# Low parts of the weights made by accumulating transfers, and an S5 step with one scan whose state ScalarE copies

## Chip, core and metric

One NeuronCore of a Trainium2 chip runs the whole program. The metric is the device time in microseconds (us) of one execution. The engines are named as the profile names them: PE (TensorE), DVE (VectorE), ACT (ScalarE), POOL (GpSimd), and SP, which here only issues DMA transfers.

## The reference

A hybrid block of two layers works on 512 latent tokens and 256 context tokens of width 1024, in float32. Each layer does an adaptive RMS norm, one wide input projection (`h @ w_in`, 6656 columns), three token mixers of width 512 whose columns come from that projection, a gated merge, an output projection and a residual add:

```python
q, k, v, za, xr, zr, us, zs, gl = split(h @ w_in)
ya = diff_attention(q, k, v)              # 4 heads, differential softmax
yr = rglru(depthwise_conv(xr))            # h[t] = a[t] h[t-1] + b[t], both directions
ys = s5(us)                               # complex diagonal state space, both directions, GLU
y  = [ya * silu(za), yr * silu(zr), ys * silu(zs)]
x  = x + gate * (sum(sigmoid(g) * (y_n @ w_branch_n)) @ w_out)
```

The S5 branch has 32 groups of 16 channels with 64 complex states each. Each state obeys h[t] = a h[t-1] + B u[t] with a constant complex a, once forwards and once backwards over the tokens; latent tokens start from the last state of the context.

## The kernel before

**Products in three parts.** Every weight product runs on PE in a rounded 32-bit format, and each operand is split into a high part and a low part so that the result is float32-like. For activations this gives hH and hL. For weights the helper `wsplit` (line 152) loads a block of 128x512 into `raw`, ACT writes the high part (`wh`, line 160) and DVE subtracts to get the low part:

```python
S.activation(wh, raw, AF.Copy)
V.tensor_sub(wl, raw, f32(wh))
```

`product` (line 164) then runs, for each of four k tiles of a block, the passes wh x hH, wh x hL and wl x hH, each over 512 latent and 256 context tokens: 24 matmuls a block, of which the fifth is the first that reads wl. The tiles wr, wh and wl have three buffers each (the four blocks of the LRU have one).

**The S5 stage.** In each layer the LRU branch (`lru(i)`, four of them), gate projections, `merge_y`, the first branch projection and the 16 steps of S5 are interleaved as the table PLAN says. In the first layer this stage follows the projection of the S5 input, at about 85 us, and ends at about 390 us; in the second it lies about 1030 to 1240 us. In the first layer the S5 tables and weights are made within the stage, on DVE (lines 442 to 515); in the second they are loaded.

**One S5 step.** The sequence is cut into 96 chunks of 8 tokens, so a scan runs over 96 elements. `s5_scan(pa)` (line 592) handles two groups in both directions. 16 matmuls on PE write the chunk inputs px (line 601), 128 partitions (two groups of 64 states) by 2 x 2 x 96 (real and imaginary, two directions). On DVE: the inputs are turned by the angle table into xx (lines 611 to 614), four real scans with the constant decay rho run in place, one for each direction and part (line 618), and the result is turned back: U2 and W2 (lines 623 and 624), then four half-height operations write the state tile st, which has real parts in partitions 0 to 63 and imaginary ones in 64 to 127 for one group each:

```python
V.tensor_sub(st[0:64, g, ...], U2[ps, 0, ...], W2[ps, 1, ...])      # line 628, g = 0, 1
V.tensor_add(st[64:128, g, ...], U2[ps, 1, ...], W2[ps, 0, ...])    # line 629
```

In the first layer one more copy (line 631) repeats 32 columns of st. `s5_out(pa)` (line 633) multiplies st and the inputs on PE into ps_y; ACT copies that to yo (line 647) and SP stores it. `step(pa)` issues the scan of pa + 1 ahead of the output of pa; there are two st tiles, one xx.

**Order.** Each engine runs its own list of instructions in order. The lists are laid down when the program is built, by the framework's planner, which may put independent instructions of one engine in another order than the program text has: in the trace parts of an S5 step stand between parts of an LRU. Transfers are issued by SP, which is also an in-order list, or by POOL. In the first layer's S5 stage POOL issues nothing; it issues transfers later, when the second layer's S5 tables are stored (lines 452 to 527).

Of the kernel before, what the change touches and what calls it, by code (L numbers as in the profile page):

```python
# [11 lines left out]
F32 = mybir.dt.float32  # L12
F32R = mybir.dt.float32r
AF = mybir.ActivationFunctionType
OP = mybir.AluOpType
# [14 lines left out]
NCH = 96  # L30
NCC = 32
# [20 lines left out]
def hybrid_kernel(ctx, tc, xT, cc, wmod, win, winv, wbr, wout, wglu, wlru, par, lqk, s5a, s5b, s5B, s5C, dsk, rope, outT):  # L52
    nc = tc.nc
    V, S, G, PE, SP = nc.vector, nc.scalar, nc.gpsimd, nc.tensor, nc.sync
# [30 lines left out]
    def f32(ap):  # L85
        return ap.bitcast(F32)
# [20 lines left out]
    ones = pC.tile([128, 32], F32, name="ones")  # L107
# [41 lines left out]
        return mods[:, l, 4 + k // 4, k % 4, c:c + 1]  # L149


    def wsplit(src, n, p=None, bufs=3, keep=None):
        p = p or pW
        raw = p.tile([128, 512], F32, name="wr", tag="wr", bufs=bufs)
        if keep:
            p, bufs = keep, None
        wh = p.tile([128, 512], F32R, name="wh", tag="wh", bufs=bufs)
        wl = p.tile([128, 512], F32R, name="wl", tag="wl", bufs=bufs)
        SP.dma_start(raw, src)
        S.activation(wh, raw, AF.Copy)  # L160
        V.tensor_sub(wl, raw, f32(wh))  # L161
        return wh.rearrange("p (k n) -> p k n", n=n), wl.rearrange("p (k n) -> p k n", n=n)

    def product(blocks, rhs, segs, out, first=True, last=True):
# [72 lines left out]
    rho = pC.tile([128, L * 32], F32, name="rho")  # L237
# [310 lines left out]
    def s5_make(l):  # L548
        need = l < L - 1
        s5st, p5 = pool(f"s5{l}", 1, side="right")  # L550
        usd = pD.tile([512, 8, NCE], F32, name=f"usd{l}")
        yd = pD.tile([512, 8, NCH], F32, name=f"yd{l}")
        NCL = NCH if need else NCH - NCC
        sts = [p5.tile([128, 2, 2, NCE], F32, name=f"st{i}", tag=f"st{i}") for i in range(2)]
        vts, sps, tps = {}, {}, {}
        if l == 0:
            pr_ = s5_params(l, p5, S5_BUFS, V)
# [34 lines left out]
        def s5_scan(pa):  # L592
            pr = pa % 4
            vt, (tb, ws) = vts[pa // 4], turn(pa)

            px = mis("ps_x")
            for d in range(2):
                for c in range(2):
                    for g in range(2):
                        v = vt[:, 2 * pr + g, :NCH] if d == 0 else vt[:, 2 * pr + g, NCE - 1:NCE - 1 - NCH:-1]  # L600
                        PE.matmul(px[64 * g:64 * g + 64, (c * 2 + d) * NCH:(c * 2 + d + 1) * NCH],  # L601
                                  lhsT=ws[:, 2 * d + g, 64 * c:64 * c + 64], rhs=v, start=True, stop=True)
            pxv = px[:, :4 * NCH].rearrange("p (c d j) -> p c d j", c=2, d=2)

            sh = [128, 2, 2, NCH]
            Cb = tb[:, 0].unsqueeze(1).to_broadcast(sh)
            Sb = tb[:, 1].unsqueeze(1).to_broadcast(sh)
            U = p5.tile([128, 2, 2, NCH], F32, name="U", tag="U")
            Wt = p5.tile([128, 2, 2, NCH], F32, name="W", tag="W")
            xx = p5.tile([128, 2, 2, NCH], F32, name="xx", tag="xx")  # L610
            V.tensor_mul(U, pxv, Cb)
            V.tensor_mul(Wt, pxv, Sb)
            V.tensor_add(xx[:, 0], U[:, 0], Wt[:, 1])
            V.tensor_sub(xx[:, 1], U[:, 1], Wt[:, 0])
            for d in range(2):
                b = l * 32 + 2 * pa + d
                for c in range(2):
                    V.tensor_tensor_scan(xx[:, c, d], rho[:, b:b + 1].to_broadcast([128, NCH]), xx[:, c, d], 0.0,
                                         op0=OP.mult, op1=OP.add)
            U2 = p5.tile([128, 2, 2, NCH], F32, name="U2", tag="U")  # L620
            W2 = p5.tile([128, 2, 2, NCH], F32, name="W2", tag="W")
            js = slice(0 if need else NCC - 1, NCH - 1)
            V.tensor_mul(U2[..., js], xx[..., js], Cb[..., js])
            V.tensor_mul(W2[..., js], xx[..., js], Sb[..., js])
            st = sts[pa % 2]
            for g in range(2):
                ps = slice(64 * g, 64 * g + 64)
                V.tensor_sub(st[0:64, g, :, js.start + 1:NCH], U2[ps, 0, :, js], W2[ps, 1, :, js])
                V.tensor_add(st[64:128, g, :, js.start + 1:NCH], U2[ps, 1, :, js], W2[ps, 0, :, js])
            if need:  # L630
                V.tensor_copy(st[:, :, 0, NCH:], st[:, :, 0, :NCC])

        def s5_out(pa):

# [25 lines left out]
        def ahead():  # L660
            for st in sts:
                V.memset(st[:, :, :, 0:1], 0.0)
            if l > 0:
                for p in range(3):
                    fetch(p)
                return
            whole(pr_.powers())
            s5_inner(0)
            done[0] = 1
            whole(pr_.tables(0))  # L670
# [22 lines left out]
    for l in range(L):  # L693
# [23 lines left out]
        for k in range(KT):  # L717
# [7 lines left out]
            b = pH.tile([128, TT], F32R, name="hL", tag="hL")  # L725
# [52 lines left out]

        if l == 0:
            s5.ahead()  # L780


        def lru(i):
# [131 lines left out]
        for dt in range(KT):  # L915
# [2 lines left out]
            V.scalar_tensor_tensor(m_t[dt][:, :W], m_t[dt][:, :W], 1.0, pb[:, :W], op0=OP.add, op1=OP.mult)  # L918
            gate_early(2, dt)
        s5.close()  # L920


        s5t, p6 = pool(f"s5t{l}", 4, side="right")
# [2 lines left out]
        for i in range(4):  # L926
            a = p6.tile([128, 8, NCL], F32, name="gt", tag="gt")
            SP.dma_start(a, s5.yd[i * 128:(i + 1) * 128, :, :NCL])
            b = p6.tile([128, 8 * NCL], F32R, name="gtH", tag="gtH")
            c = p6.tile([128, 8 * NCL], F32R, name="gtL", tag="gtL")  # L930
# [9 lines left out]
        for n in range(4):  # L940
            wh, wl = wsplit(wglu[l, n].rearrange("p k n -> p (k n)"), 128)
# [80 lines left out]
        for h in range(4):  # L1022
# [5 lines left out]
            for q0 in ([0, 2, 4] if need else [0, 2]):  # L1028
# [5 lines left out]
                for qi in range(2):  # L1034
# [3 lines left out]
                    for c in range(2):  # L1038
# [4 lines left out]
                        for t0, w, c0 in ks:  # L1043
# [12 lines left out]
                                           op1=OP.add)  # L1056
# [246 lines left out]
```

## Time and profile before

| what | value |
|---|---|
| median of 3 runs | 1617.53 us (1614.93 to 1617.88) |
| profiled execution, its own time | 1609.46 us |
| its span, first to last instruction | 1607.6 us |
| busy over the span: PE, DVE, ACT, POOL | 93%, 73%, 47%, 8% |
| mean granted clock of PE | 0.973 of full speed |

A busy share is an average over stages, so it says little about any one of them; the views by stage further down do. "Idle before, releaser" in a row is the time for which the engine stood still ahead of these instructions and which event ended it. PE's granted clock has two levels, 1.2 and 2.4 GHz; 1.00 means that the higher one was granted all the time.

### The profile page before, as it was taken

How to read it: one execution, taken by the hardware profiler on the slowest of the kernel's cores; microseconds unless marked ns; L12 is line 12 of the kernel's file. 1: busy time of each engine (PE TensorE's matmuls, PEld its weight loads, DVE VectorE, ACT ScalarE, POOL GpSimd, SP SyncE). 2: the span in 40 equal slices, each digit the busy share in tenths (PEclk: the TensorE clock that was granted, in tenths of full speed). 3: DMA queues.
4: the chain of work that ended last, by engine and by line, in shares of the span. 5: the costliest groups of instructions: out<-in, count | busy, mean ns of one | idle time of the engine just before them, and what ended most of it. 6: DMA issues, size and time to landing. Idle time of an engine off the chain costs nothing. (4 is left out here: it accounts for less than half of the span.)

```text
span 1607.6 us, 24547 instructions
## 1 busy us (share of the span) xinstructions
PE 1496.6 (93%) x9096; PEld 1253.3 (78%) x9096; DVE 1171.6 (73%) x2463; ACT 751.9 (47%) x1300; POOL 126.0 (8%) x175
## 2 busy tenths in 40 slices
PE   4997569999999999999898999899899999999997
PEld 2786448888888898888777888777788988888877
DVE  6799999985447756677888875479876478488555
ACT  7573425533334434543233455576624355355433
POOL 0000000000000000000534320000000000000120
PEclk9999779999999999999999999999999999999999
DMA  8532112132211111113575662445454322211442
GB/s 282 163 99 69 38 52 74 36 105 83 73 60 40 53 46 47 46 40 126 196 250 177 232 224 69 130 138 158 127 157 132 99 66 59 66 60 60 152 162 93
DMA packets 103144, 174.43 MB, mean 109 GB/s; under 512 B 24432, under 2 KB 41456, under 8 KB 103024
## 3 DMA queue, kind: packets, MB, share of 16 engines
q1 hardware_dynamic: 97392, 158.17, 31.4%
q0 software_dynamic: 5632, 14.69, 2.7%
q8 instruction: 72, 1.18, 0.3%
q14 instruction: 48, 0.39, 0.1%
HBM read 145.02 MB, written 25.69 MB: 106 GB/s over the span
## 5 line engine op out<-in xcount | busy, mean ns | idle before, releaser
L160 ACT ACTIVATE wh<-wr 128x512 fp32r<-128x512 f32 x320 | 200.0, 630 | 409.4 <-PE ps_in L174 193.9
L174 PE MATMUL ps_in<-hH,wh 128*128 128x512 f32 x1248 | 374.8, 358 | 11.3 <-ACT m L839 4.8
L174 PE MATMUL ps_in<-hH,wl 128*128 128x512 f32 x1248 | 376.8, 358 | 8.8 <-DVE wl L161 8.8
L174 PE MATMUL ps_in<-hL,wh 128*128 128x512 f32 x1248 | 371.4, 356 | 0.0
L161 DVE TENSOR_TENSOR wl<-wr,wh 128x512 fp32r<-128x512 f32 x320 | 226.3, 711 | 181.4 <-ACT wh L160 134.9
L174 PEld LDWEIGHTS ps_in<-hH,wh 128*128 128x128 f32 x1248 | 205.9, 190 | 49.0 <-ACT m L839 5.6
L174 PEld LDWEIGHTS ps_in<-hH,wl 128*128 128x128 f32 x1248 | 207.5, 190 | 43.4 <-DVE wl L161 10.1
L174 PEld LDWEIGHTS ps_in<-hL,wh 128*128 128x128 f32 x1248 | 205.0, 190 | 31.6 <-issue 0.2
L884 POOL TENSOR_TENSOR m<-m,g 128x768 f32<-128x768 f32 (+1 forms) x16 | 34.2, 2135 | 1104.1 <-DVE rc L1052 426.1
L1049 ACT ACTIVATE p<-ps_s,mx 128x768 f32<-128x768 f32 (+1 forms) x80 | 65.2, 816 | 71.4 <-DVE mx L1048 67.5
L174 PE MATMUL ps_b<-yH,wh 128*128 128x512 f32 (+1 forms) x288 | 88.3, 357 | 0.0
L174 PE MATMUL ps_b<-yH,wl 128*128 128x512 f32 (+1 forms) x288 | 87.9, 357 | 0.0
L174 PE MATMUL ps_b<-yL,wh 128*128 128x512 f32 (+1 forms) x288 | 87.8, 357 | 0.0
L1047 DVE TENSOR_REDUCE mx<-ps_s 128x1 f32<-128x768 f32 (+1 forms) x80 | 67.6, 847 | 23.6 <-PE ps_s L1044 22.9
L174 PEld LDWEIGHTS ps_b<-yH,wh 128*128 128x128 f32 x288 | 47.9, 188 | 9.7 <-issue 1.7
L174 PEld LDWEIGHTS ps_b<-yH,wl 128*128 128x128 f32 x288 | 47.7, 188 | 7.4
L174 PEld LDWEIGHTS ps_b<-yL,wh 128*128 128x128 f32 x288 | 47.6, 188 | 7.3
L174 PE MATMUL acc<-mH,wh 128*128 128x512 f32 (+1 forms) x160 | 49.4, 340 | 0.0
L174 PE MATMUL acc<-mH,wl 128*128 128x512 f32 (+1 forms) x160 | 49.1, 338 | 0.0
L174 PE MATMUL acc<-mL,wh 128*128 128x512 f32 (+1 forms) x160 | 48.9, 338 | 0.0
L1041 PE MATMUL ps_s<-ks,qs 128*128 128x256 f32 (+1 forms) x144 | 42.5, 367 | 3.3 <-ACT ks L1015 1.5
L174 PE MATMUL ps_g<-uHL,wh 128*128 128x512 f32 (+1 forms) x128 | 34.5, 384 | 11.5 <-ACT uHL L803 7.3
(349 smaller groups left out, 2823.3 us busy)
## 6 DMA issues: line engine op xcount, KB each, us to landing
wr<-in_win SPq DMA_DIRECT2D x208, 256.0 KB
wm<-in_wmod SPq DMA_DIRECT2D x48, 512.0 KB
wr<-in_wbr SPq DMA_DIRECT2D x48, 256.0 KB
sp<-s5d SPq DMA_DIRECT2D x16, 768.0 KB
wr<-in_wout SPq DMA_DIRECT2D x32, 256.0 KB
s5d<-vv POOLq DMA_DIRECT2D x16, 320.0 KB, 3.7
usd<-up SPq DMA_DIRECT2D x8, 512.0 KB
vt<-usd SPq DMA_DIRECT2D x64, 64.0 KB
```

The source lines that it names most:

```text
L160: S.activation(wh, raw, AF.Copy)
L161: V.tensor_sub(wl, raw, f32(wh))
L174: PE.matmul(out[:, c0:c0 + n], lhsT=(wl if ps == 2 else wh)[:, k, :], rhs=rhs(k0 + k, ps == 1)[:, t0:t0 + n], start=st, stop=en)
L884: (V if n == 0 and dt >= ADD_V[l] else G).tensor_add(m_t[dt][:, :W], m_t[dt][:, :W], g[:, :W])
L1041: PE.matmul(sc[:, c0:c0 + w], lhsT=qs[:, c, qt * 128:(qt + 1) * 128], rhs=kk[:, c, t0:t0 + w], start=True, stop=False)
L1047: V.reduce_max(mx[:, 0:1], sc[:, :kw], axis=AX.X)
L1049: S.activation(p[c][:, :kw], sc[:, :kw], AF.Exp, bias=mx[:, 1:2], scale=0.125, accum_out=sm[:, c:c + 1])
```

## The change

In the first layer's S5 stage, from the first LRU to the last branch projection, `wsplit` makes the low part otherwise: ACT writes -wh into wl, and a transfer issued by POOL adds raw to it in place. In S5 steps of both layers the four scans become one scan over 384 elements, with a tile dec of decays: rho in columns 1 to 95 of each of the four sections, and 0 in column 0, where a new section begins. ACT writes dec in each step (two instructions of 2 x 95 elements). The back-turned state is written into xx, full height, by two DVE operations, and ACT copies it to st in four half-height copies; the copy of 32 columns moves to ACT as well. xx gets two buffers.

```diff
+    by_dma = [False]
...
         S.activation(wh, raw, AF.Copy)
-        V.tensor_sub(wl, raw, f32(wh))
+        if by_dma[0]:
+            S.activation(wl, f32(wh), AF.Copy, scale=-1.0)
+            G.dma_start(wl, raw, accum_op=OP.add)
+        else:
+            V.tensor_sub(wl, raw, f32(wh))
...
+        dec = p5.tile([128, 2, 2, NCH], F32, name="dec", tag="dec")
...
-            xx = p5.tile([128, 2, 2, NCH], F32, name="xx", tag="xx")
+            xx = p5.tile([128, 2, 2, NCH], F32, name="xx", tag="xx", bufs=2)
+            for d in range(2):
+                b = l * 32 + 2 * pa + d
+                S.activation(dec[:, :, d, 1:], ones[:, 0:1].unsqueeze(2).to_broadcast([128, 2, NCH - 1]), AF.Copy,
+                             scale=rho[:, b:b + 1])
...
-            for d in range(2):
-                b = l * 32 + 2 * pa + d
-                for c in range(2):
-                    V.tensor_tensor_scan(xx[:, c, d], rho[:, b:b + 1].to_broadcast([128, NCH]), xx[:, c, d], 0.0,
-                                         op0=OP.mult, op1=OP.add)
+            xf = xx.rearrange("p c d j -> p (c d j)")
+            V.tensor_tensor_scan(xf, dec.rearrange("p c d j -> p (c d j)"), xf, 0.0, op0=OP.mult, op1=OP.add)
...
+            V.tensor_sub(xx[:, 0, :, js], U2[:, 0, :, js], W2[:, 1, :, js])
+            V.tensor_add(xx[:, 1, :, js], U2[:, 1, :, js], W2[:, 0, :, js])
             for g in range(2):
-                ps = slice(64 * g, 64 * g + 64)
-                V.tensor_sub(st[0:64, g, :, js.start + 1:NCH], U2[ps, 0, :, js], W2[ps, 1, :, js])
-                V.tensor_add(st[64:128, g, :, js.start + 1:NCH], U2[ps, 1, :, js], W2[ps, 0, :, js])
+                for c in range(2):
+                    S.activation(st[64 * c:64 * c + 64, g, :, js.start + 1:NCH], xx[64 * g:64 * g + 64, c, :, js], AF.Copy)
             if need:
-                V.tensor_copy(st[:, :, 0, NCH:], st[:, :, 0, :NCC])
+                S.activation(st[:, :, 0, NCH:], st[:, :, 0, :NCC], AF.Copy)
...
         def ahead():
             for st in sts:
                 V.memset(st[:, :, :, 0:1], 0.0)
+            V.memset(dec[:, :, :, 0:1], 0.0)
...
         if l == 0:
             s5.ahead()
+
+        by_dma[0] = l == 0
...
         s5.close()
+        by_dma[0] = False
```

## Rows read from the trace of the kernel before

**Rows 1.** Windows: span, length, busy us (instructions) per engine, granted clock, DMA share, GB/s
```profile
85.00:120.00 35.00, 34.04 (x259) 28.16 (x259) 34.30 (x74) 25.17 (x41) 0.00 (x0) 1.00 0.34 97
120.00:260.00 140.00, 97.20 (x659) 80.00 (x658) 129.26 (x310) 58.03 (x99) 0.00 (x0) 0.80 0.20 55
260.00:395.00 135.00, 132.40 (x871) 113.95 (x870) 111.54 (x224) 59.73 (x97) 0.00 (x0) 1.00 0.26 75
790.00:960.00 170.00, 158.90 (x1077) 131.28 (x1078) 143.21 (x303) 66.97 (x147) 64.33 (x120) 0.97 0.65 216
1030.00:1225.00 195.00, 184.41 (x1102) 151.18 (x1099) 163.30 (x347) 104.62 (x146) 0.00 (x0) 0.98 0.45 136
```

**Rows 2.** Waits, 120 to 260 us: who waited for whom, total, times, longest
```profile
PE ps_in L174 <- DVE wl L161: 7.5, 1, 7.5
PE ps_wt L522 <- DVE wt L515: 7.4, 2, 5.6
```

**Rows 3.** Groups by line, VectorE, 120 to 260 us: busy us, mean ns, idle before
```profile
L618 DVE TENSOR_TENSOR_SCAN xx<-rho,xx 128x96 f32<-128x96 f32 x35 | 9.9, 336 | 0.0
L161 DVE TENSOR_TENSOR wl<-wr,wh 128x512 fp32r<-128x512 f32 x13 | 8.8, 686 | 0.1
...
L629 DVE TENSOR_TENSOR st<-U,W 64x190 f32<-64x190 f32 x16 | 5.6, 352 | 0.2
L628 DVE TENSOR_TENSOR st<-U,W 64x190 f32<-64x190 f32 x16 | 5.5, 345 | 0.1
```

**Rows 4.** The same view, VectorE, 85 to 120 us
```profile
L618 DVE TENSOR_TENSOR_SCAN xx<-rho,xx 128x96 f32<-128x96 f32 x10 | 3.0, 340 | 0.0
...
L161 DVE TENSOR_TENSOR wl<-wr,wh 128x512 fp32r<-128x512 f32 x3 | 2.0, 673 | 0.0
```

**Rows 5.** Timeline of VectorE, 241 to 257 us: start us, duration us, instruction
```profile
241.25 0.34 DVE L628 TENSOR_TENSOR st<-U,W 64x190 f32<-64x190 f32 x1
...
242.72 0.69 DVE L161 TENSOR_TENSOR wl<-wr,wh 128x512 fp32r<-128x512 f32 x1
243.32 0.19 DVE L631 COPY st<-st 128x64 f32<-128x64 f32 x1
243.43 0.68 DVE L161 TENSOR_TENSOR wl<-wr,wh 128x512 fp32r<-128x512 f32 x1
...
255.26 0.35 DVE L614 TENSOR_TENSOR xx<-U,W 128x192 f32<-128x192 f32 x1
255.53 1.09 DVE L618 TENSOR_TENSOR_SCAN xx<-rho,xx 128x96 f32<-128x96 f32 x4
256.54 0.67 DVE L515 TENSOR_TENSOR wt<-wt,wu 128x512 f32<-128x512 f32 x1
```

**Rows 6.** One line's instructions: the LRU's scan of 512, ns min/median/max
```profile
L829 DVE TENSOR_TENSOR_SCAN ysum<-r,ysum,gi x8: 1256/1257/1261, 122.2 to 1153.7; 128x512 f32<-128x512 f32 x8
```

**Rows 7.** Groups by line, ScalarE, 85 to 345 us
```profile
L160 ACT ACTIVATE wh<-wr 128x512 fp32r<-128x512 f32 x34 | 20.8, 626 | 40.2 <-PE ps_in L174 37.0 <-DMA wr<-in_win 2.1 <-issue 1.1
...
L823 ACT ACTIVATE a<-r 128x1536 f32<-128x1536 f32 x4 | 5.9, 1482 | 0.0
...
L647 ACT ACTIVATE yo<-ps_y 128x192 f32<-128x192 f32 x14 | 4.6, 327 | 34.9 <-PE ps_y L643 34.9
```

**Rows 8.** Timeline of VectorE, first layer's last branch projections
```profile
380.88 0.95 DVE L918 SCALAR_TENSOR_TENSOR m<-m,ps_b 128x768 f32<-128x768 f32 x1 [2.60 <-PE ps_b L174]
...
385.04 0.95 DVE L918 SCALAR_TENSOR_TENSOR m<-m,ps_b 128x768 f32<-128x768 f32 x1 [2.60 <-PE ps_b L174]
```

**Rows 9.** One line's instructions: POOL's 256 KB transfers of line 527
```profile
L527 POOL DMA_DIRECT2D s5d<-ws x16: 542/556/622, 794.9 to 954.5; - x16
...
DMA to landing us min/median/max: 2.3/3.0/6.6
```

**Rows 10.** Waits, second layer's S5 stage, 1030 to 1225 us
```profile
DVE wl L161 <- ACT wh L160: 17.7, 11, 4.1
```

**Rows 11.** Groups by line, VectorE, 1030 to 1225 us
```profile
L628 DVE TENSOR_TENSOR st<-U,W 64x128 f32<-64x128 f32 x32 | 9.1, 284 | 0.6
```

## The prediction before the run

> **What bounds the kernel now.** I read the views in the order in which the rows stand. First the busy time by stage [rows 1]. Over the whole run PE looks like the bound, but that is a mean. From 120 to 260 us, inside the first layer's S5 stage, PE is busy 97.2 of 140 us and its granted clock is 0.80 on the mean, so it is idle 42.8 us and part of the rest runs at the lower of its two levels. VectorE is busy there 129.3 of 140 us, ScalarE 58.0, POOL not at all. From 260 to 395 the picture is turned round: PE 132.4 of 135. In the second layer's S5 stage (1030 to 1225) PE has 184.4 of 195 and VectorE 163.3. So VectorE sets the time in one stretch of 140 us, and hardly anywhere else that the change touches.
>
> Then the waits of that stretch [rows 2]: PE waits 7.5 us for a low part (wl) and 7.4 us for wt, both VectorE's; the first had its weight long before and stood behind an S5 step in VectorE's queue. Third, which VectorE work of the stretch the change takes away [rows 3, 4]. Last, what such an instruction really occupies: the durations overlap, so I go by starts [rows 5].
>
> **The change part by part.**
>
> *Low parts.* One wl holds VectorE from 242.72 to 243.32, 0.60 us [rows 5], less than its mean of 0.686 [rows 3]. 13 stand in 120 to 260 and 3 in 85 to 120 [rows 3, 4]: 16 x 0.60 = 9.6 us off VectorE. The 44 of the whole stage would be 26 us, but those after 260 lie where PE is the bound, and are worth at most PE's idle 2.6 us there [rows 1]; I count 0.
>
> *Scans.* Four scans of 96 hold VectorE from 255.53 to 256.54, 1.01 us [rows 5]. One of 384 lies between 0.336 us for 96 [rows 3] and 1.257 for 512 [rows 6]: 0.336 + 288 x 0.921/416 = 0.97 us, less the 0.08 by which neighbours overlap (0.68 of duration against 0.60 of occupation): 0.89. Saved 0.12. Bounds: below, nothing, if each of the 384 costs what one does in the short form (then 1.01); above 0.4, were the short scans never overlapped (4 x 0.336 = 1.34 against 0.97).
>
> *State.* Four half-height writes hold VectorE from 241.25 to 242.72, 1.47 us; two full-height operations of 190 elements are like the 192-element ones, 255.26 to 255.53, 0.27 each: 0.54. The copy (243.32 to 243.43, 0.11) goes too [rows 5]. Saved 1.04; with the scan 1.16 a step. 120 to 260 holds 32 of the half-height writes, 8 steps [rows 3]; 85 to 120 holds 10 scans, 2.5 steps [rows 4]. 10.5 x 1.16 = 12.2 us.
>
> Together 21.8 us off VectorE before 260, 4.7 of them before 120 (3 x 0.60 + 2.5 x 1.16). PE is busy 34.0 of 35 us before 120, so those 4.7 pay only because they shorten the backlog with which VectorE enters the stretch; I count them whole.
>
> *ScalarE.* From 0.626 us for 512 elements and 1.482 for 1536 [rows 7], 190 elements cost 0.626 - 322 x 0.836/1000 = 0.36. A step adds two dec writes and four state copies, 2.1 us, and a copy of 64, 0.25: about 2.4; a low part adds 0.63. In 120 to 260: 8 x 2.4 + 13 x 0.63 = 27 us on 58.0 busy of 140. There is room, so the work itself costs nothing; with the stretch shortened to 120 us ScalarE would be 71% busy.
>
> *The new waits.* The scan now waits for dec, which ScalarE writes; the state copies on ScalarE wait for VectorE, and what is queued behind them (yo, wh, ws, strip, all wanted by PE) waits with them. dec is one tile, so it is written after the previous step's scan. The trace has no such link. Below: nothing, when ScalarE is idle at that moment, as it is for 82 of 140 us. Above: ScalarE spends 34.9 us over 14 yo waiting for PE [rows 7], 2.5 us each; a dec behind each of those holds VectorE 2.5 x 10.5 = 26 us. The nearest ordinary thing in front of it is one wh, 0.63 us: 10.5 x 0.63 = 6.6 us. I take that, as the other end needs the worst order in every step.
>
> *The transfers.* Chain from raw weight to wl: wh 0.63, negated copy 0.63, transfer D. Where PE is the bound, three buffers let wh(n) start when PE is done with block n-3. A block takes 380.88 to 385.04, 4.16 us [rows 8]; wl is first used at the 5th of its 24 matmuls, so 20/24, 3.47 us, follow. PE doesn't notice while 0.63 + 0.63 + D + 3.47 stays under 3 x 4.16 = 12.48, that is D under 7.75 us. Nearest row: POOL's 256 KB transfer of ws to memory lands after 2.3, 3.0 and 6.6 us (fastest, median, slowest) [rows 9]. This one reads two tiles and adds, so from 2.3 to twice the slowest, 13.2. I take 3 to 6: hidden by two blocks of PE's work. POOL is empty in this stage, so nothing is queued behind. The raw tile is held D longer; its next load then still has 12.48 - 1.26 - 6 = 5.2 us. The cover gone, each microsecond of D above 7.75 costs a third per block: 24 such blocks before 395, so 8 us per microsecond.
>
> On POOL's transfers the trace shows that the 3.0 us stand in a stretch with VectorE busy 143 of 170 us [rows 1, 9], nearly all of it two-input operations as here. The Trainium skill (SBUF — State Buffer, the box on the trap "DVE blocks DMA") says that a POOL-issued DMA can't get its descriptors written while VectorE runs a 2-port mode, and gives about 620 ns against 3100 ns. By that I estimate D at 3.0 + 2.5 = 5.5, under the limit as well; the sum stays, but D then has half the reserve, and I put the slow rival's chance at 0.18 where the rows alone would have had 0.15.
>
> *Second layer.* VectorE loses 0.12 and about 1.14 - 0.5 a step (the 64x128 writes are 0.284 [rows 11]), ScalarE gains 2.0 (two dec of 0.36, four copies of 128 at 0.31). PE bounds it; its idle 10.6 us [rows 1] limit a gain, and against it low parts there already wait 17.7 us for wh on ScalarE [rows 10], which now has 16 x 2.0 = 32 us more in front. I count 0, between -7 and +10 (16 x 0.63).
>
> **Sum.** -21.8 + 6.6 = -15.2 us. Against the profiled execution's 1609.46 that is 1594.3. The median of the three runs stands 8.07 above that execution, so 1602.3; I say 1602. Its own range: half the gain (-7.6) to one without the new wait (-21.8), widened by 3: 1593 to 1613.
>
> **The rivals.**
>
> 1. *VectorE's relief is worth more than its time.* For: PE idles 42.8 us at a low clock; a wl no longer stands behind S5. VectorE's own 10.7 idle us of the stretch come from PE being late, and could go too: -21.8 - 10.7 = -32.5, so 1585. Against: they need the new waits to be free. Chance 0.12.
> 2. *The new waits eat it.* dec behind yo in most steps: 21.8 - 26 to 21.8 - 16, so between -6 and +4; about 1617. For: yo's waits are ScalarE's largest there. Against: it needs the planner to put dec late. Chance 0.15.
> 3. *The transfer sets the pace (slower).* If adding makes D long, PE in 260 to 395 waits for wl. It decides from D = 7.75; the gain is gone at 7.75 + 15.2/8 = 9.65; at 11 the loss is 26 and the sum +10.8: 1628. Against: it needs over three times the median of [rows 9]. Chance 0.18.
> 4. *The second layer pays (slower).* The state now reaches PE by way of ScalarE, in a stage bound by PE: +10 there, and half the gain in the first layer kept: 1620. Chance 0.07.
>
> The forecast has 0.48.
>
> **How the numbers follow.** The kernel's runs differ by 0.18%, so 0.2%, 3.2 us, is what can be told from no change. Faster: 0.48 + 0.12 + 0.02 of rival 2 = 0.62. Same: 0.11 of rival 2, 0.02 of rival 4: 0.13. Slower: 0.18 + 0.05 + 0.02: 0.25. The range goes from rival 1's 1585 to rival 3's 1628, which leaves out its longer D.
>
> **What would show it.** Right: in the stretch after 120 us VectorE keeps over 85% busy but the stage's last merge comes some 15 us sooner; PE idle under 30 us and clock over 0.80; scans of 384 near 0.97 us; D under 7; after the S5 stage PE as before. Wrong: PE matmuls with wl waiting for a DMA (rival 3), VectorE scans waiting for ScalarE's dec by more than 1 us each (rival 2), ps_y waiting for ScalarE's st in the second layer (rival 4).

## The result, and the profile after

The changed kernel takes 1589.45 us (median of 4 runs, 1587.38 to 1594.94) against 1616.26 (4 runs, 1614.93 to 1617.88) for the kernel before: ratio 0.9839, 95% interval 0.9809 to 0.9869, so 1.6% faster. The prediction said 1602, with a range of 1585 to 1628 over the forecast and its rivals: the side and that range are right, the size is not, since 26.8 us were gained where 15.2 were forecast. The time lies just below the forecast's own range, 1593 to 1613.

The profiled execution takes 1587.50 us (span 1585.7) against 1609.46 (span 1607.6), so it shows 22.0 us of the gain. Where they lie, by four marks in the two traces: the last merge of the first layer's branch projections (the end of [rows 8]), the last store of the first layer's output to memory, the same merge in the second layer, and the end of the span.

| stretch | before, us | after, us | difference |
|---|---|---|---|
| start to the first layer's last merge | 385.0 | 351.5 | -33.5 |
| from there to the first layer's last store | 590.4 | 595.1 | +4.7 |
| from there to the second layer's last merge (its S5 stage lies here) | 260.6 | 267.5 | +6.9 |
| from there to the end | 371.6 | 371.6 | 0 |

The second line is not the change's: nothing in that stretch was touched, and over the twelve kernels run below it is 591 to 599 us, without any order by edit. The first and the third are the two halves of this study. The first is over twice the forecast, the third was forecast at 0.

The end of the first layer's stage in VectorE's timeline of the changed kernel (start us, duration us, instruction) answers to [rows 8]. The distance of two merges is the same 4.16 us, so PE's pace at the end is what it was; only the time at which it gets there has moved, by 385.04 - 351.51:

```profile
347.35 0.95 DVE L932 SCALAR_TENSOR_TENSOR m<-m,ps_b 128x768 f32<-128x768 f32 x1 [2.60 <-PE ps_b L180]
351.51 0.95 DVE L932 SCALAR_TENSOR_TENSOR m<-m,ps_b 128x768 f32<-128x768 f32 x1 [2.60 <-PE ps_b L180]
```

The windows of the changed kernel answer to [rows 1] (same columns: span, length, busy us and instructions of PE, PEld, DVE, ACT, POOL, granted clock, DMA share, GB/s):

```profile
85.00:120.00 35.00, 33.97 (x260) 28.11 (x259) 29.85 (x57) 30.01 (x56) 2.56 (x3) 1.00 0.51 122
120.00:260.00 140.00, 124.93 (x889) 103.80 (x888) 128.87 (x278) 106.93 (x217) 20.06 (x24) 0.96 0.52 118
260.00:395.00 135.00, 129.67 (x828) 112.02 (x827) 89.52 (x147) 75.19 (x130) 11.87 (x14) 0.97 0.42 102
1030.00:1225.00 195.00, 183.70 (x1040) 150.53 (x1041) 138.48 (x239) 122.09 (x218) 0.00 (x0) 0.97 0.44 132
```

From 120 to 260 PE is now busy 124.9 us instead of 97.2, at a granted clock of 0.96 instead of 0.80, and it gets through 889 matmuls instead of 659. VectorE is as busy as before there (128.9 against 129.3): its stretch isn't emptied, it is refilled with work from later. ScalarE goes from 58.0 to 106.9.

PE's waits in the changed kernel, 85 to 352 us (who waited for whom, total us, times, longest us), answer to [rows 2]:

```profile
PE ps_in L180 <- ACT wh L162: 7.3, 3, 3.7
PE ps_in L180 <- DMA wl<-wr: 4.9, 5, 2.3
PE ps_y L651 <- DVE W L624: 4.5, 1, 4.5
```

The waits for wl and wt as VectorE's work are gone. What is late next is ScalarE's wh, and five times the transfer.

The transfer's line, and the new scan's line with what it waited for (ns min/median/max, first and last start; idle time of the engine before it by releaser, us and times):

```profile
L165 POOL DMA_DIRECT2D wl<-wr x44: 850/859/1210, 65.3 to 342.8; - x44
...
DMA to landing us min/median/max: 3.2/3.9/6.0
```

```profile
L628 DVE TENSOR_TENSOR_SCAN xx<-dec,xx x32: 931/954/960, 98.9 to 1193.6; 128x384 f32<-128x384 f32 x32
...
its engine sat idle before it (us, times) until:
  ACT dec L621: 0.3, 1
who waited for it (us, times):
  ACT dec L621: 9.9, 11
```

The transfer lands after 3.9 us, inside the 3 to 6 that the prediction took. The scan waited for dec once, 0.3 us in all 32 steps: the wait that was counted at 6.6 us does not exist. It points the other way: ScalarE's dec waits for VectorE's previous scan, 9.9 us in all.

What one step occupies, in VectorE's timeline of the changed kernel, answers to [rows 5]:

```profile
222.04 0.95 DVE L628 TENSOR_TENSOR_SCAN xx<-dec,xx 128x384 f32<-128x384 f32 x1
222.91 0.80 DVE L472 TENSOR_TENSOR vv<-vv,vu 128x640 f32<-128x640 f32 x1
...
226.22 0.35 DVE L635 TENSOR_TENSOR xx<-U,W 128x190 f32<-128x190 f32 x1
226.49 0.35 DVE L636 TENSOR_TENSOR xx<-U,W 128x190 f32<-128x190 f32 x1
226.75 0.68 DVE L842 TENSOR_TENSOR_SCAN ysum<-r,gi 128x256 f32<-128x256 f32 x1
```

Start to start, the scan holds VectorE 0.87 us (forecast 0.89) and the two back-turn operations 0.27 and 0.26 (forecast 0.27 each). The sizes of VectorE's instructions were right to a few hundredths of a microsecond. On ScalarE (groups of the changed kernel, 85 to 352 us: busy us, mean ns, idle before), which answer to [rows 7], dec takes 0.44 where 0.36 was estimated:

```profile
L162 ACT ACTIVATE wh<-wr 128x512 fp32r<-128x512 f32 x43 | 26.5, 624 | 27.9 <-PE ps_b L180 12.4 <-PE ps_in L180 9.5 <-DMA wr<-in_win 5.8
L164 ACT ACTIVATE wl<-wh 128x512 fp32r<-128x512 f32 x40 | 24.6, 623 | 0.4
L640 ACT ACTIVATE st<-xx 64x190 f32<-64x190 f32 x64 | 23.0, 359 | 3.8 <-DVE xx L635 3.2
L621 ACT ACTIVATE dec<-ones,rho 128x190 f32<-128x190 f32 x30 | 12.1, 440 | 3.7 <-DVE xx L628 3.7
```

### The profile page after: what moved, and what is told of

It is laid out like the page before. It is cut to its first block, busy times and chain, and to the rows that moved or that the text cites. A ratio compares the mean times of both kernels' runs of the same rounds, so it can differ in the third digit from the quotient of the medians.

```text
span 1585.7 us, 24730 instructions
## 1 busy us (share of the span) xinstructions
PE 1492.8 (94%) x9096; PEld 1249.5 (79%) x9096; DVE 1118.3 (71%) x2245; ACT 841.8 (53%) x1552; POOL 163.6 (10%) x219
## 5 line engine op out<-in xcount | busy, mean ns | idle before, releaser
L167 DVE TENSOR_TENSOR wl<-wr,wh 128x512 fp32r<-128x512 f32 x276 | 194.9, 710 | 186.5 <-ACT wh L162 142.0
L165 POOL DMA_DIRECT2D wl<-wr x44 | 38.1, 893 | 246.6 <-ACT wl L164 193.9
L640 ACT ACTIVATE st<-xx 64x190 f32<-64x190 f32 (+1 forms) x128 | 42.7, 333 | 10.3 <-DVE xx L635 8.6
```

Of the source, the lines that this page charges most:

```text
L165: G.dma_start(wl, raw, accum_op=OP.add)
L640: S.activation(st[64 * c:64 * c + 64, g, :, js.start + 1:NCH], xx[64 * g:64 * g + 64, c, :, js], AF.Copy)
```

## The experiments

Three sets of four kernels; those of a set ran on one chip beside the kernel before. "Stage 1" is the end of the first layer's S5 stage (385.0 before, 351.5 after), "stage 2" the third line of the table above (260.6 and 267.5). Both are from one profile each, and kernels that have the same code in a stage differ there by up to 5 us: the seven kernels with the changed first layer end it between 351.5 and 356.1, the seven with the second layer's old step have 259.5 to 264.1. Smaller differences of length are not read. PE's idle time in a stage, its length less PE's busy time, varies less (in the second layer 13.0 to 13.7 us in those seven kernels), so it is read as well.

### The changed kernel again, beside its parts

> The changed kernel again, beside the three next ones, so that they can be set against it on the same chip. Main theory (T): the first layer's S5 stage is some 33 us shorter, the second layer's some 7 longer, the total 22 to 27 us below the kernel before, ratio about 0.984. Its rival would be a ratio outside 0.981 to 0.987, with which the first timing would have been an accident.

Measured: 1593.73 us against 1613.22, ratio 0.9872 (0.9851 to 0.9894). Stage 1 351.6, stage 2 270.4. Both halves of the result come back, the second layer's loss a little larger.

### The transfers alone

The S5 step is the one before; only the low parts change.

```diff
-            V.tensor_tensor_scan(xf, dec.rearrange("p c d j -> p (c d j)"), xf, 0.0, op0=OP.mult, op1=OP.add)
+            for d in range(2):
+                b = l * 32 + 2 * pa + d
+                for c in range(2):
+                    V.tensor_tensor_scan(xx[:, c, d], rho[:, b:b + 1].to_broadcast([128, NCH]), xx[:, c, d], 0.0,
+                                         op0=OP.mult, op1=OP.add)
...
-            V.tensor_sub(xx[:, 0, :, js], U2[:, 0, :, js], W2[:, 1, :, js])
-            V.tensor_add(xx[:, 1, :, js], U2[:, 1, :, js], W2[:, 0, :, js])
             for g in range(2):
-                for c in range(2):
-                    S.activation(st[64 * c:64 * c + 64, g, :, js.start + 1:NCH], xx[64 * g:64 * g + 64, c, :, js], AF.Copy)
+                ps = slice(64 * g, 64 * g + 64)
+                V.tensor_sub(st[0:64, g, :, js.start + 1:NCH], U2[ps, 0, :, js], W2[ps, 1, :, js])
+                V.tensor_add(st[64:128, g, :, js.start + 1:NCH], U2[ps, 1, :, js], W2[ps, 0, :, js])
```

> Only the low parts by transfers, S5 steps as before. T: VectorE's relief is what counts, and of the 43.6 us that left VectorE in the first layer's stage the low parts are 44 x 0.60 = 26, so the stage gains 33.5 x 26 / 43.6 = 20 us, the second layer's stage stays as before; total about 20 below the kernel before (ratio 0.988). Rival R1 (what counts is that a wl no longer stands behind an S5 step in VectorE's queue; the step's own part is worth nothing): the stage gains all 33, total 33 below (0.980).

Measured: 1584.32 us, ratio 0.9816 (0.9795 to 0.9837): faster than the whole change on the same chip. Stage 1 354.2, so 30.8 of the 33.5 us; stage 2 263.5. The low parts carry the first layer's gain, and the rest of the change is what costs time in the second layer.

### The S5 step alone

```diff
-        by_dma[0] = l == 0
+        by_dma[0] = False
```

> Only the S5 step's part (one scan, state moved by ScalarE), in both layers, all low parts by VectorE. T: 16 x 1.16 = 18.6 us leave VectorE in the first layer, gain 33.5 x 18.6 / 43.6 = 14 us there, and the second layer's stage costs 7: total 7 below the kernel before (0.996). R1: nothing gained in the first layer, 7 lost in the second: 7 above (1.004).

Measured: 1616.47 us, ratio 1.0012 (0.9998 to 1.0025): nothing. Stage 1 376.9, a gain of 8.1; stage 2 270.2, and the gain is given back there and on the way.

### The new step in the first layer only

```diff
-            xf = xx.rearrange("p c d j -> p (c d j)")
-            V.tensor_tensor_scan(xf, dec.rearrange("p c d j -> p (c d j)"), xf, 0.0, op0=OP.mult, op1=OP.add)
+            if l == 0:
+                xf = xx.rearrange("p c d j -> p (c d j)")
+                V.tensor_tensor_scan(xf, dec.rearrange("p c d j -> p (c d j)"), xf, 0.0, op0=OP.mult, op1=OP.add)
+            else:
+                for d in range(2):
...
```

The writes of dec and of the state take the same branch, and the second layer has one buffer of xx again.

> The changed kernel with the second layer's S5 steps as before. T: the 7 us that the second layer's stage lost come from the ScalarE work that the step adds there, so this one is 7 us below the changed kernel, about 29 to 34 below the kernel before (0.979 to 0.982). Rival R2: the 8.3 us stall of one px in the second layer is an accident of that profile or of the list, not the step's doing: within 2 us of the changed kernel.

Measured: 1580.48 us, ratio 0.9803 (0.978 to 0.9826), the fastest of all kernels here: 13.3 us below the changed kernel on the same chip, with an interval that doesn't touch the changed kernel's. Its interval does overlap that of the transfers alone, 3.8 us above it, so the two can't be told apart. Stage 1 351.6, stage 2 263.8. So the new step in the second layer costs time, against the forecast of 0. The two profiles are 11.3 us apart: 6.5 of them lie in that stage, and 4.6 in the two stretches where both kernels have the same code.

### Is it VectorE's time, or the place in its queue?

The transfers alone, and VectorE does a subtraction of the size of the old low part at the same place, into a tile that nobody reads:

```diff
             G.dma_start(wl, raw, accum_op=OP.add)
+            scr = pW.tile([128, 512], F32, name="scr", tag="scr", bufs=1)
+            V.tensor_sub(scr.rearrange("p (k n) -> p k n", n=128), f32(wh).rearrange("p (k n) -> p k n", n=128),
+                         ident.unsqueeze(1).to_broadcast([128, 4, 128]))
```

> Transfers only (S5 steps as before), and VectorE does for each of the 44 low parts a subtraction of the same size all the same, from wh and the identity into a scratch tile that nobody reads. VectorE has its 26 us back, but no PE work waits for them. Theory Q (a wl stood behind S5 and LRU work in VectorE's queue; PE gains because it no longer waits there): the stage still ends near 354 us, total near the 1584 of the transfers alone, at most 5 more. Theory V (VectorE's time is the bound, each us taken off is a us gained): the stage ends near 380 to 385, total 1608 to 1613.

Measured: 1616.42 us, ratio 1.0007 (0.9985 to 1.0029); stage 1 385.9. The whole 30.8 us are gone, although the low parts come from the transfer and no matmul waits directly for a VectorE instruction to get its wl. What PE waits for instead is VectorE's other work, by the waits of this kernel, 85 to 386 us:

```profile
ACT wh L162 <- DVE scr L167: 21.8, 4, 9.9
...
PE ps_y L652 <- DVE st L641: 10.3, 2, 6.1
PE ps_in L183 <- DMA wl<-wr: 8.9, 5, 3.3
...
PE ps_wt L531 <- DVE wt L524: 6.9, 3, 4.9
PE ps_st L487 <- DVE vv L475: 6.3, 2, 4.2
```

Three of the four largest waits of PE are products of VectorE that the edit didn't touch. So it is the instructions on VectorE that cost the time, wherever the lateness comes out, and taking the wl out of its queue gains nothing while others of its size stand there. Two things are left in this test. The dummy reads wh, so wh's buffer is held until it has run (the first line): ScalarE stands still for it three times for 5 us or more, until 178.9, 251.4 and 311.0 us. In the first two PE stands still too, but what ends its wait is VectorE's st (6.1 and 4.2 us); in the third PE runs on. After the first of them PE's longest wait for a transferred wl is 2.5 us, so this link shows little of the 30.8 directly. And the planner lays out the lists with the dummies in them: from 176 to 262 us PE's list holds 131 of the product's ps_in matmuls with the dummies, 152 in the kernel before and 328 with the transfers alone. Whether VectorE's time on the chip or the order that the planner makes of it gives the gain was not separated; no run keeps the order and changes the time. The dummy's group (VectorE, 85 to 386 us: busy us, mean ns, idle before) has the duration of the low parts of [rows 3]:

```profile
L167 DVE TENSOR_TENSOR scr<-wh,ident 128x512 f32<-128x512 f32 x40 | 27.3, 682 | 3.3 <-ACT wh L162 3.0
```

The stage as a whole, from 85 us to its end, in five kernels (windows, columns as above). The kernel before:

```profile
85.00:385.00 300.00, 253.65 (x1727) 213.45 (x1727) 270.06 (x599) 139.77 (x231) 0.00 (x0) 0.91 0.24 69
```

with the dummies:

```profile
85.00:385.90 300.90, 257.91 (x1725) 217.27 (x1724) 269.26 (x600) 161.29 (x271) 35.05 (x41) 0.90 0.46 105
```

the transfers alone:

```profile
85.00:354.20 269.20, 244.57 (x1727) 206.19 (x1726) 243.67 (x555) 162.02 (x271) 35.04 (x41) 0.96 0.51 117
```

the step alone:

```profile
85.00:376.90 291.90, 254.03 (x1721) 214.43 (x1720) 251.95 (x502) 176.08 (x341) 0.00 (x0) 0.91 0.25 71
```

and the changed kernel:

```profile
85.00:351.50 266.50, 245.07 (x1722) 205.82 (x1722) 226.88 (x457) 196.85 (x381) 34.49 (x40) 0.97 0.51 118
```

VectorE's busy time falls by 26.4 us with the transfers (270.1 to 243.7) and the stage by 30.8; its idle time (length less busy) is 30, 32 and 26 us in the first three. In the changed kernel it falls by another 17 us and the stage by 2.7: its idle time rises to 40, and PE, busy 245.1 of 266.5, has little left to give.

### Half of the transfers: the early ones, the late ones

Transfers alone, switched off from the last LRU of the stage on (21 low parts), or switched on only there (23).

```diff
+            if i == 3:
+                by_dma[0] = False
             ysum.append(lru(i))
```

> Transfers only, and only for the first three LRUs and the gates and S5 steps between them (21 of the 44 low parts); from the fourth LRU on VectorE subtracts as before. The prediction's step (VectorE work after 260 us counts nothing): the same as with all 44, 1584, stage end near 354. If the late ones count by their time: 23 x 0.6 = 14 more, 1598.

Measured: 1603.51 us, ratio 0.9928 (0.9901 to 0.9956); stage 1 377.2, a gain of 7.9.

```diff
-        by_dma[0] = l == 0
...
+            if i == 3:
+                by_dma[0] = l == 0
             ysum.append(lru(i))
```

> Transfers only, and only from the fourth LRU to the end of the stage (23 of the 44). The prediction's step: nothing gained, 1613, stage end near 385. If late ones count by their time: 14 less, 1599.

Measured: 1616.66 us, ratio 1.0021 (1.0003 to 1.0038); stage 1 388.1. The late low parts alone are worth nothing, the early ones alone 8 us, both together 31. VectorE's busy time over the stage falls by 10.4 us with the early ones and by 11.4 with the late ones, so the first are gained nearly at their time and the second not at all. Why they don't add up is seen from 176 to 262 us. Before:

```profile
176.00:262.00 86.00, 61.52 (x422) 51.08 (x423) 78.38 (x193) 34.38 (x63) 0.00 (x0) 0.76 0.19 53
```

the early transfers only:

```profile
176.00:262.00 86.00, 58.22 (x410) 48.20 (x409) 78.76 (x198) 34.87 (x66) 2.58 (x3) 0.72 0.25 59
```

all of them:

```profile
176.00:262.00 86.00, 85.16 (x632) 72.17 (x631) 84.81 (x214) 52.69 (x96) 13.82 (x16) 1.00 0.57 129
```

With the early ones alone the stretch looks as it did before (PE 58 of 86 us, clock 0.72): only 3 transfers and 3 low parts by VectorE fall into it. PE does not wait there for a low part of VectorE's but for its other products (PE's waits, 176 to 262 us):

```profile
PE ps_wt L528 <- DVE wt L521: 11.1, 3, 7.4
PE ps_y L649 <- DVE st L638: 8.3, 1, 8.3
```

With all of them 16 transfers fall into it and PE is busy 85 of 86 us at full clock. The S5 steps are no faster for it: 96 of their ps_x matmuls stand in the stretch in either kernel, and VectorE is busy 79 and 85 us. What differs is how many product matmuls PE has between them (groups, 176 to 262 us, one of the three passes; the early transfers, then all):

```profile
L180 PE MATMUL ps_in<-hL,wh 128*128 128x512 f32 x20 | 8.2, 412 | 0.0
L180 PE MATMUL ps_in<-hL,wh 128*128 128x512 f32 x55 | 21.7, 394 | 0.0
```

So blocks whose low parts stood after 262 have come forward into the stretch in which VectorE is short, and fill PE's waits for it. PE's list is in order and laid down at build time, so this is the planner's order for the relieved VectorE.

### What in the second layer costs time: the scan, the state, or the queue of ScalarE

New step in the first layer only, and in the second layer the one scan with dec:

```diff
             else:
                 for d in range(2):
                     b = l * 32 + 2 * pa + d
-                    for c in range(2):
-                        V.tensor_tensor_scan(xx[:, c, d], rho[:, b:b + 1].to_broadcast([128, NCH]), xx[:, c, d], 0.0,
-                                             op0=OP.mult, op1=OP.add)
+                    S.activation(dec[:, :, d, 1:], ones[:, 0:1].unsqueeze(2).to_broadcast([128, 2, NCH - 1]), AF.Copy,
+                                 scale=rho[:, b:b + 1])
...
+            V.tensor_tensor_scan(xf, dec.rearrange("p c d j -> p (c d j)"), xf, 0.0, op0=OP.mult, op1=OP.add)
```

> Against the new step in the first layer only: the second layer too has one scan with decays written by ScalarE, but VectorE writes its state as before. 2 x 0.44 = 0.88 us a step on ScalarE. Theory A: 0.88 of 2.1 us a step, so 3 to 4 us longer, total about 1584. Theory L with dec as the link: most of the 7 to 10.

Measured: 1583.8 us, ratio 0.9813 (0.9783 to 0.9844); stage 2 263.0, PE idle in it 15.8.

Or the state by way of ScalarE, with the four scans:

```diff
             else:
-                for g in range(2):
-                    ps = slice(64 * g, 64 * g + 64)
-                    V.tensor_sub(st[0:64, g, :, js.start + 1:NCH], U2[ps, 0, :, js], W2[ps, 1, :, js])
-                    V.tensor_add(st[64:128, g, :, js.start + 1:NCH], U2[ps, 1, :, js], W2[ps, 0, :, js])
+                V.tensor_sub(xx[:, 0, :, js], U2[:, 0, :, js], W2[:, 1, :, js])
+                V.tensor_add(xx[:, 1, :, js], U2[:, 1, :, js], W2[:, 0, :, js])
...
```

> Against the new step in the first layer only: in the second layer ScalarE copies the state, with four scans as before. 4 x 0.31 = 1.24 us a step on ScalarE. Theory A: 4 to 5 us longer, total about 1585. Theory L with the copies as the link: most of the 7 to 10.

Measured: 1585.68 us, ratio 0.9825 (0.979 to 0.986); stage 2 263.1, PE idle in it 16.0. Neither half by itself lengthens the stage by anything that shows: both are like the 263.8 of the old step. PE's idle time is 2 to 3 us above the old step's 13.0 to 13.7.

Or the old step in the second layer, with six ScalarE instructions of the size of the new step's beside it, into a tile that nobody reads:

```diff
+                scr = p5.tile([128, 2, 2, NCH], F32, name="scr", tag="scr")
+                for d in range(2):
+                    b = l * 32 + 2 * pa + d
+                    S.activation(scr[:, :, d, 1:], ones[:, 0:1].unsqueeze(2).to_broadcast([128, 2, NCH - 1]), AF.Copy,
+                                 scale=rho[:, b:b + 1])
+                for g in range(2):
+                    for c in range(2):
+                        S.activation(scr[64 * c:64 * c + 64, g, :, 1:65], st[64 * c:64 * c + 64, g, :, NCC:NCH], AF.Copy)
```

> The new step in the first layer only; in the second the step is as before (four scans, state written by VectorE), but ScalarE does for each step six operations of the same sizes as the new step's (two of 190 elements, four of 64x128) into a scratch tile that nobody reads. Theory A (ScalarE's time in front of the LRU chain costs the second layer's stage its 7 to 10 us): the second layer's stage is as long as in the changed kernel, 267 to 270 us from the last x1d store to its last branch projection, total about 1587 to 1592. Theory L (the new links cost it: scan behind dec, PE's ps_y behind ScalarE's copies): 261 to 264 us, total within 3 of the kernel without the dummies, 1580.

Measured: 1591.59 us, ratio 0.9853 (0.9818 to 0.9888); stage 2 267.8. That is 4 us more than the old step's 263.8, within the spread of one profile, but all runs (1589.04 to 1593.86) lie above those of the scan alone on the same chip (1582.32 to 1587.48). The stage from the first layer's last store to its end, PE's idle time being the length less PE's busy time (windows, columns as above), with the new step, then with the old step in the second layer, then with the dummies:

```profile
946.10:1216.46 270.36, 250.65 (x1441) 206.62 (x1439) 172.72 (x302) 166.25 (x289) 0.00 (x0) 0.96 0.41 125
943.00:1206.85 263.85, 250.73 (x1441) 207.90 (x1439) 183.59 (x382) 137.08 (x195) 0.00 (x0) 0.96 0.42 128
950.90:1218.66 267.76, 250.47 (x1441) 206.61 (x1439) 184.95 (x383) 165.17 (x289) 0.00 (x0) 0.96 0.41 126
```

PE's busy time is the same to 0.3 us, and its idle time is 19.7, 13.1 and 17.3 us. So ScalarE's added work by itself brings about 4 of the 6 us that the whole new step costs PE, though nobody waits for the dummies' results. The dummies are not free of links, however: their four copies read st, and ScalarE stands still for VectorE's st ahead of them for 9.2 us in all, in five times. The link of the scan to dec and that of PE to the copies are what they lack.

### The other half of the first layer's step

The transfers, and in the first layer the state by way of ScalarE with the four scans of before; the second layer's steps are the old ones.

```diff
-            V.tensor_tensor_scan(xf, dec.rearrange("p c d j -> p (c d j)"), xf, 0.0, op0=OP.mult, op1=OP.add)
+            for d in range(2):
...
```

> A version meant to be the fastest: transfers in the first layer's stage, there also the state copied by ScalarE but four scans as before (the one scan saves VectorE 0.12 us a step and costs ScalarE 0.88), the second layer's steps as before. If VectorE's time alone counts: 2 us slower than with the one scan, 1582. If ScalarE's time counts as well by now: 1 to 3 us faster, 1578.

Measured: 1582.74 us, ratio 0.9809 (0.9778 to 0.9839); stage 1 353.0. With the transfers alone it was 354.2, with the whole step 351.5 to 356.1: what scan and state bring on top of the transfers can't be told from the spread. PE's idle time from 85 us to the stage's end is 24.6 us with the transfers alone, 22.8 here and 20.3 to 22.3 with the whole step, which leaves the step some 2 to 4 us at most.

### Transfers in the second layer too

```diff
-        by_dma[0] = l == 0
+        by_dma[0] = True
```

> The new S5 step in the first layer only, transfers for the low parts in the S5 stages of both layers. In the second layer's stage PE is the bound and wl waits for wh on ScalarE (17.7 us), not for VectorE. Theory V or Q alike: within 4 us of the same without them (1580). A rival: the transfers free wl there too and PE's 10 idle us go: 1572. Another: 44 x 0.63 us more on ScalarE delay the LRU chain, as the S5 step did: 1587.

Measured (new step in the first layer only): 1602.68 us, ratio 0.9926 (0.9887 to 0.9964); stage 2 276.4, which is 12.6 us more than without. There VectorE isn't what is short: it waits for ScalarE's wh already [rows 10], and the negated copy gives ScalarE 0.62 us more for each block. PE's idle time in the stage doubles, from 13.1 to 26.1 us, and its largest wait is now for the transfer itself (PE's waits, 1000 to 1235 us):

```profile
PE ps_in L180 <- DMA wl<-wr: 10.4, 7, 2.5
```

How much of the loss is ScalarE's added copies and how much the transfers themselves stays open; no run takes the copy alone.

## Why the prediction was right, and where it was wrong

**The bound: right.** VectorE's instructions set the first layer's S5 stage. The dummies give the whole gain back (385.9 against 385.0), and PE's waits then stand at VectorE's other products. That it is their time on the chip, and not the planner's order for them, is argued.

**The low parts: the step that failed.** "Those after 260 lie where PE is the bound ... I count 0": 9.6 us were counted and the transfers alone bring 30.8. Two things bear on it. The first is the row. The window of 260 to 395 [rows 1] is a mean over two states, as finer windows of the kernel before show (columns as in [rows 1]):

```profile
262.00:312.00 50.00, 48.47 (x334) 40.96 (x333) 48.94 (x114) 27.59 (x43) 0.00 (x0) 1.00 0.20 58
312.00:350.00 38.00, 36.94 (x261) 31.67 (x260) 36.63 (x78) 13.38 (x26) 0.00 (x0) 1.00 0.26 71
350.00:386.00 36.00, 36.00 (x218) 31.81 (x217) 19.88 (x29) 13.95 (x20) 0.00 (x0) 1.00 0.36 113
```

VectorE is 97% busy until 350; PE is alone only in the last 36 us. But PE is as busy there (85.4 of the 88 us from 262 to 350, at full clock), so the 2.6 us at which the prediction capped those low parts hold where they stand. What failed is the second, the cut by time. Late low parts by themselves are worth nothing, as the prediction said, but once the early ones are gone the late ones come forward into the stretch in which VectorE is short. A cut at a time of the old trace holds for one instruction taken away, not for a class of them that runs through the stage. The 44 of the whole stage, times 0.60 us, are the 26 us that the prediction worked out and set aside; VectorE's busy time fell by 26.4.

The stage gave 30.8 for these 26.4, more than their time. PE's granted clock over the stage went from 0.91 to 0.96, and PE's busy time from 253.7 to 244.6 us for the same 1727 matmuls; the other 21.7 us are idle time of PE. Rival 1 had its head right, that the relief is worth more than its time. Its 32.5 us, near what the first layer gave, are luck: they add VectorE's 10.7 idle us from 120 to 260, and with the whole change VectorE is idle there for 11.1.

**The new waits: 6.6 us counted, 0.3 measured.** The bound from below was the right end. dec itself has to wait only for the previous scan, and ScalarE had it written before VectorE came to the scan in 31 of 32 steps. The row of wh behind which dec was supposed to stand says how long such a thing takes, not that it stands there.

**The step: 12.2 us counted, 8.1 alone, nothing certain on top of the transfers.** The sizes were right, but it isn't added to the other term: with the transfers PE is at 91% of the stage (244.6 of 269.2), and 17 us more off VectorE end as VectorE's idle time.

**ScalarE in the first layer: right.** Its busy time in the stage rises from 140 to 197 us and PE's waits for wh are 7.3 us.

**The transfers: right.** 3.9 us, at most 6.0, under the limit of 7.75 (one of the 44 in the kernel with the transfers alone took 8.4); rival 3 falls, though the wait by which it would have shown is there, with 4.9 us in five. The trap of the Trainium skill (SBUF — State Buffer, the box on "DVE blocks DMA"), by which D was estimated at 5.5, doesn't show: VectorE is busy 227 of 267 us in the stage, and the median transfer is 0.9 us over the plain one of [rows 9]. The same page of the Trainium skill (section Who interferes with whom) says that a VectorE instruction with two SBUF inputs takes its second one through the shared read interface, and, marked there as inferred, that tensor_tensor doesn't take the write interface that generating descriptors needs. All but some 2 us of VectorE's work here has two inputs, and the 3.9 us agree with that. No run here has one-input copies in their place.

**The second layer: counted 0, measured +6.9, within the stated -7 to +10 and near rival 4's +10.** Rival 4 named the place, not the link. In ScalarE's timeline of the changed kernel the new work stands among the LRU's gates (lines 827 to 837):

```profile
1112.09 0.45 ACT L621 ACTIVATE dec<-ones,rho 128x190 f32<-128x190 f32 x1
1112.44 0.89 ACT L827 ACTIVATE r<-ps_g,prm 128x768 f32<-128x768 f32 x1
...
1114.49 0.30 ACT L640 ACTIVATE st<-xx 64x128 f32<-64x128 f32 x1
1114.75 0.90 ACT L827 ACTIVATE gi<-ps_g,prm 128x768 f32<-128x768 f32 x1
1115.55 1.02 ACT L835 ACTIVATE r<-r,c 128x768 f32<-128x768 f32 x1
1116.58 0.63 ACT L640 ACTIVATE st<-xx 64x128 f32<-64x128 f32 x2
```

VectorE waits for the end of these gates, 6.76 us where the kernel before has 3.41 at the same place:

```profile
1120.61 1.76 DVE L839 SCALAR_TENSOR_TENSOR gi<-gi,u 128x1536 f32<-128x1536 f32 x1 [6.76 <-ACT gi L827]
...
1135.80 0.56 DVE L623 TENSOR_TENSOR U<-ps_x,sp 128x384 f32<-128x384 f32 x1
```

VectorE's other wait for ScalarE, that of the low parts [rows 10], is not the step's doing: from the first layer's last store to the stage's end it is 35.7 us in the changed kernel and 35.7 in the one with the old step there. Rival 4's own sign, ps_y waiting for ScalarE's st, is 0.5 us in all.

VectorE's LRU work then runs late, the next step's product stands behind it until 1135.80, and PE, which wants that step's PSUM buffer, stands still:

```profile
1136.93 1.51 PE L609 MATMUL ps_x<-vt,sp 128*64 128x96 f32 x14 [8.32 <-DVE W L624]
```

The stall is in both profiles of the changed kernel and in that of the step alone (8.3 to 8.4 us), and in none of the other eleven. It is not the loss by itself: the kernels with half of the step have single stalls of 7.2 and 7.0 us at other places (PE for VectorE's st, PE for its sz), and a stage like the old one's. PE's idle time over the stage orders the kernels better: 13.0 to 13.7 us with the old step (seven profiles), 15.8 and 16.0 with half of the new, 17.3 with the dummies, 19.4 to 19.7 with the whole (three profiles). It rises with ScalarE's busy time, 137 us, then 147 and 155, then 165 and 166. So most of the loss goes with ScalarE's added time (2.1 us a step: two of 0.44 and four of 0.31). The 2 us between the dummies and the whole step may be the links' or those of the order in which the planner puts the new items; one profile of the dummies doesn't settle it.

**The sum.** -21.8 + 6.6 + 0 was forecast and -33.5 + 6.9 measured, beside 4.7 that are no part of it. The errors had both signs, which is why the total came out within the range: without the 6.9 and the 4.7 us the time would have been about 1578, below its 1585. That part is luck. The signs that the prediction named came as said for VectorE's share after 120 us (92%), PE's idle time there (15 us), its clock (0.96), the scan (0.95 us) and D; they failed for the last merge (33 us sooner, not 15) and for the second layer.

## What to carry to other kernels

Before a class of instructions is counted at 0 in part of a stage, ask what moves into the place of what is taken away, and split that part until the engines' shares stop changing; a dummy of equal size that nobody reads then shows in one run whether the engine still pays (look at what its inputs hold up, and at the order of the lists). Work moved to an idle engine is paid for wherever that engine feeds a chain: put the new step only where the relieved engine is short. In lengths that vary by 5 us, the bound engine's idle time can show what the length hides. The version with the new step in the first layer alone has the best median here (ratio 0.9803 against 0.9872 for the changed kernel beside it), but the transfers alone (0.9816) can't be told from it and need no new step.

## What the runs showed of the hardware that was not expected

An accumulating 256 KB transfer within SBUF landed in 3.9 us, only 0.9 more than the plain one to memory of [rows 9], while POOL spent 0.86 us on issuing it against 0.56. And ScalarE's dec write, 190 elements from one broadcast value with its scale from a column of rho, took 0.44 us where copies of 190 elements from a half-height tile took 0.36, so the estimate from long instructions was 0.08 short. Which of the differences makes it was not tested.
